# One quarter of the first modulation columns is moved between two products of the second weight pair

## The chip, the core and the metric

The kernel runs on one core of one Trainium2 chip. A core has a matrix engine (TensorE, PE in the profile; its weight loads are shown apart as PEld), a vector engine (VectorE, DVE), a scalar engine (ScalarE, ACT), a general engine (GpSimd, POOL) and a queue that issues transfers (SyncE, SP). Each engine works through its own instructions in order and waits for the others by semaphores. The metric is the device time of one execution in microseconds (us); less is better.

## The reference, cut to what matters

One decoder layer is computed for 512 prompt tokens and for 64 sample tokens (8 sequences of 8), all with 1024 features. Nine vectors c (one for the prompt, eight for the samples) give, through the matrix `w_ada`, nine chunks of 1024 modulation values; the first two chunks, `sh1` and `sc1`, are the shift and scale of the first feed-forward block.

```python
m = jax.nn.silu(c) @ w_ada + b_ada
sh1, sc1, g1, sh2, sc2, g2, sh3, sc3, g3 = jnp.split(m[:, None, :], N_MOD, axis=-1)
h = modulate(rms_norm(x, n1_g), sh1, sc1)          # n * (1 + scale) + shift
x = x + 0.5 * g1 * swiglu(h, w1_gate, w1_up, w1_down)
...                                                 # token mixing, then a second feed-forward block
```

`swiglu` is `(silu(h @ w_gate) * (h @ w_up)) @ w_down` with 2816 hidden columns, all in float32.

## The kernel before

**Layout.** Activations lie with features on the 128 partitions, in 8 chunks of 128 features, and with the 576 tokens as columns; the columns are cut into two halves of 288. Weights are taken 128 columns at a time, one block of `w_gate` and the same block of `w_up`; such a couple is a "pair". To keep float32 accuracy each operand is split into a high and a low part (ACT makes the high part, DVE the low part), and a product is three matmuls for each chunk: high by high, high by low, low by high. The function `prod` is one product over four chunks: 12 matmuls with 288 columns (profile line L651).

**Blocks.** The features are cut into an upper half (chunks 0 to 3) and a lower half (4 to 7), the tokens into two halves; this gives operand blocks such as N11 (upper features, first tokens, negated), N1 (a difference of the upper blocks), B21 and B22 (the lower features), and sums T2, N3, N4 for later pairs. Index j in a step's name is which two chunks: the steps ending in 0, 1 work on the upper half, the B21 and B22 steps ending in 2, 3 on the lower half. The steps ending in `h` plus a number write the high part on ACT (L564, L566), those in `l` the low part on DVE (L571, L575). The first two weight pairs, `pairs[0]` and `pairs[1]` of class `Plain`, use four steps of two products each:

- `h0a`: the pair's two weight blocks n11 (gate) and n21 (up) by N11, into two PSUM banks `A`;
- `snaps` (`sn0`, `sn1`): ACT copies both banks aside (L660);
- `h1a`: the same weights by N1, into two banks `D`;
- `h0b`: the blocks a12 and a22 by B21, added into `A`; `h1b`: the same by B22, added into `D`.

There are eight PSUM banks.

**The first modulation columns.** They come in four quarters, class `First`, each 256 columns of `sh1` and 256 of `sc1`. Quarter 3 serves the feature chunks 6 and 7. Each quarter has eight loads of 256 KB (L363) and four steps: `mm` is 16 matmuls on PE over the eight weight tiles (L307), `M` an ACT copy of the result from PSUM (L313), `tr` four transposes on PE (L319), and `m` three DVE instructions that finish the values (L324, L328, L387). With them the steps `b30` and `b31` (ACT, L540) and `s3` (DVE, L549) modulate the chunks 6 and 7, and only then can `N3c1` (DVE, L591), `B21h3` (ACT) and `B21l3` (DVE) make the last part of B21, and `B22h3` and `B22l3` that of B22. The weight tiles of quarter 3 lie in buffers that the operand blocks N3 (pool `xs1`, the tiles 0 to 3 of the quarter) and N4 (pool `xa`, the tiles 4 to 7) take over.

**The order.** The first stage is written out by hand in the string `BEGIN`: each word is a step. The function `run` calls the steps in this order and then adds a dependency between each instruction and the one before it on the same engine, for all engines but SP, so the order of the words is the order on PE, ACT, DVE and POOL. After `BEGIN` come the remaining pairs in a stream. Weight loads are issued by SP as buffers come free.

Of the kernel before, what the change touches and what calls it, by code (L numbers as in the profile page):

```python
# [44 lines left out]
xt0 xt1 xc0 xt2 xc1 xt3 xc2 xt4 xc3 s5 xt5 xc4 r5 r50 r51 r52 xt6 dg xc5 xt7 xc6 rw xS xc7  # L45
rr xr0 xr3 mm0 xr2 M0 tr0 xr1 mm1 m0 nh0 s0 M1 nl0 b00 tr1 b01 m1 wh0 tx0 b10 s1 b11 wl0
N11h0 N11h1 N11l0 N1h0 N11l1 mm2 tx1 N1l0 N1h1 h0a0 T2a1 M2 N1l1 nh1 T2a0 wh1 nl1 tr2 sn0
h1a0 m2 wl1 b20 b21 s2 B21h2 T2b0 B22h2 h0a1 B21l2 T2h0 N3c0 N4c0 N3h0 T2l0 N4h0 N3l0 mm3
B22l2 sn1 N4l0 M3 tr3 h1a1 m3 b30 s3 b31 B21h3 N3c1 p2ah B21l3 T2b1 h0b1 B22h3 p2al p2bh
T2h1 N3h1 N4c1 B22l3 N4h1 p2S h0b0 T2l1 p2U p2bl p2Sh N3l1 h1b0 p2V N4l1 p2Sl e0s0 e0s1 e0m0  # L50
e0m1 h1b1 e1a0 p2Uh e1t0 e1s0 p2Ul e1m0 Gh0 P1 e1a1 e1t1 e1s1 Gl0 P2 e1m1 P1s Gh1 Gl1 P5 P6
P5s P6s
# [32 lines left out]
def layer_kernel(ctx: ExitStack, tc: tile.TileContext, a):  # L85
# [24 lines left out]
    def nm(s):  # L110
        count[0] += 1
        return f"{s}_{count[0]}"
# [5 lines left out]
    def pool(stack, name, side="left"):  # L118
        return stack.enter_context(tc.tile_pool(name=nm(name), bufs=1, side=side, reuse_waits="tile"))
# [14 lines left out]
    def nine(home, shape, dt=F32R):  # L134
        return now[home].tile(shape, dt, tag="x", name=nm(home), bufs=4 if home == "xa" else 3)
# [9 lines left out]
    def bank():  # L145
        return pp.tile([P, 512], F32, tag="ps", name=nm("ps"), bufs=8)
# [85 lines left out]
    def tick(us):  # L232
        for s in list(side):
            s[1] -= us
            while s in side and s[1] <= 0:
                try:
                    s[1] += next(s[0])
                except StopIteration:
                    side.remove(s)
# [239 lines left out]
    def proj(w, X, h, kc=KC, c0=0, ks=None, ps=None):  # L479
        ps = bank() if ps is None else ps  # L480
        wh, wl = w
        for k in ks or range(kc):
            xh, xl = X[k]
            for z, (s, m) in enumerate(((wh, xh), (wh, xl), (wl, xh))):
                PE.matmul(  # L485
                    ps[:, :PW[h]], lhsT=s[:, k, c0:c0 + P], rhs=m[:, PART[h]],
                    start=k == 0 and z == 0, stop=k == kc - 1 and z == 2,
                )
        return ps
# [5 lines left out]
    def cost(kc):  # L495
        return kc * 3 * 0.1225
# [20 lines left out]
    def op(name):  # L517
        if name not in ops:
            t = nine("xs1" if name in ops["near"] else "xa", [P, 4, 2, H])
            ops[name] = t[:, :, 0], t[:, :, 1]  # L520
        return ops[name]
# [71 lines left out]
    def operand_steps(O):  # L593
        st = {}
        for j in range(2):
            for n in ("T2", "N3", "N4", "N1"):
                st[f"{n}h{j}"] = lambda n=n, j=j: O.hi(n, j)
                st[f"{n}l{j}"] = lambda n=n, j=j: O.lo(n, j)
            for n in ("B21", "B22"):
                st[f"{n}h{j + 2}"] = lambda n=n, j=j: O.hi(n, j)  # L600
                st[f"{n}l{j + 2}"] = lambda n=n, j=j: O.lo(n, j)
            st[f"N11h{j}"] = lambda j=j: O.hi("N11", j)
            st[f"N11l{j}"] = lambda j=j: O.lo("N11", j)
            st[f"tx{j}"] = lambda j=j: O.tx(j)
            for n in ("T2a", "T2b", "N3c", "N4c"):
                st[f"{n}{j}"] = lambda n=n, j=j: O.sums(n, j)
        for p in range(4):
            st[f"s{p}"] = lambda p=p: O.s(p)
        return st
# [14 lines left out]
    def pair_steps(p, greg):  # L624

        st = {}

        def G(i, f):
            if now.get("slf") is not greg:
                greg.close()  # L630
                now["sl"], now["slots"], now["slf"] = pool(greg, "slf", "right"), FSLOT, greg
            f(i)

        for i in range(2):
            for n, f in (("nh", "nh"), ("nl", "nl"), ("wh", "wh"), ("wl", "wl"), ("h0a", "h0a"), ("sn", "snaps"),
                         ("h1a", "h1a"), ("h0b", "h0b"), ("h1b", "h1b"), ("e0s", "e0s"), ("e0m", "e0m"),
                         ("e1a", "e1a"), ("e1s", "e1s"), ("e1t", "e1t"), ("e1m", "e1m")):
                st[f"{n}{i}"] = lambda i=i, f=f: getattr(p[i], f)()
            st[f"Gh{i}"] = lambda i=i: G(i, lambda i: p[i].finish_hi())
            st[f"Gl{i}"] = lambda i=i: G(i, lambda i: p[i].finish_lo())  # L640
        for n in ("p2ah", "p2al", "p2bh", "p2bl", "p2S", "p2Sh", "p2Sl", "p2U", "p2V", "p2Uh", "p2Ul"):
            st[n] = lambda n=n: getattr(p[2], n[2:])()
        for n, f in (("P1", "p1"), ("P2", "p2"), ("P5", "p5"), ("P6", "p6"), ("P1s", "p1s"), ("P5s", "p5s"), ("P6s", "p6s")):
            st[n] = lambda f=f: getattr(p[2], f)()
        return st

    def prod(ps, w, x, fresh):
        (wh, wl), (xh, xl) = w, x
        for j in range(4):
            for z, (s, m) in enumerate(((wh, xh), (wh, xl), (wl, xh))):  # L650
                PE.matmul(  # L651
                    ps[:, :H], lhsT=s[:, j * P:(j + 1) * P], rhs=m[:, j, :],
                    start=fresh and j == 0 and z == 0, stop=j == 3 and z == 2, skip_group_check=True,
                )
        tick(cost(4))
# [44 lines left out]
    class Plain(Weights):  # L700
# [21 lines left out]

        def h0a(self):
            self.A = [bank() for _ in range(2)]
            for ps, w in zip(self.A, ("n11", "n21")):
                prod(ps, self.w[w], op("N11"), True)

        def snaps(self):
            self.s = [snap(ps, half() if self.n and i else None) for i, ps in enumerate(self.A)]
# [294 lines left out]
    def cols(w, f):  # L1024
        return (w[0], f * P), (w[1], f * P)

    pairs = {0: Plain(cols(w1, 0), 0)}
# [14 lines left out]
    def turn_x(c):  # L1042
        psX[c] = bank()
        for n in range(4):
            PE.transpose(
                psX[c][:, n * P:(n + 1) * P], in_=xtok[n, c // 4][:, (c % 4) * P:(c % 4 + 1) * P], identity=ident
            )
        PE.transpose(
            psS[:, c * NS:(c + 1) * NS], in_=xtok[4, c // 4][:, (c % 4) * P:(c % 4 + 1) * P],
            identity=ident[0:NS, 0:NS],  # L1050
        )
# [37 lines left out]

    ops["near"] = ("B21", "B22", "N3")  # L1090
    steps = {**operand_steps(Late()), **pair_steps(pairs, greg)}
    for c in range(KC):
        steps[f"xt{c}"] = lambda c=c: turn_x(c)
        steps[f"xc{c}"] = lambda c=c: DVE.tensor_copy(out=xs[c][:, 0:NP], in_=psX[c])
# [733 lines left out]
    for pr in ([0], [1], [2], [3], [4], [5], [6, 7]):  # L1828
# [4 lines left out]
        for h in range(2):  # L1833
            for c in pr:
                ps = proj(W[c], OA, h)
# [44 lines left out]
    pairs = {0: Plain(cols(w2, 0), 0), 1: Plain(cols(w2, 1), 1), 2: Pair(cols(w2, 2))}  # L1880
    steps = {**operand_steps(O), **pair_steps(pairs, greg)}
# [173 lines left out]
```

## Time and profile before

| | |
|---|---|
| time, median of 3 runs | 1647.48 us (1645.12, 1647.48, 1648.8) |
| the profiled execution's own time | 1648.44 us |
| its span, first to last instruction | 1646.7 us |
| mean granted PE clock | 0.996 |
| PE busy | 1617.6 us, 98% of the span |
| PEld busy | 1554.9 us, 94% |
| DVE busy | 1152.2 us, 70% |
| ACT busy | 782.9 us, 48% |
| POOL busy | 293.0 us, 18% |

In a timeline a row is: start in us, length in us, engine, line, operation, output and inputs, shapes and count; in brackets at the end the engine's idle time ahead of the row and what is taken to have released it. Neighbouring instructions of one form are merged into one row, and since matmuls are pipelined the end of a merged row of PE can lie past the start of the next. The chain of waits is followed back from the last instruction to what released each step. A view by windows gives for each stretch of the span its length, the busy time of PE, PEld, DVE, ACT and POOL (number of instructions in brackets), the granted PE clock (1.00 is full), the busy share of the DMA engines and the GB/s that they moved. A named releaser is inferred from semaphore events; it can be a transfer that ended at the right moment while the true releaser was another.

### The profile page before, as it was taken

Reading aid. Unit: us, or ns where it says so; the run is one execution under the profiler, and the core shown is the slowest. Engines: PE = TensorE matmul, PEld = TensorE weight load, DVE = VectorE, ACT = ScalarE, POOL = GpSimd, SP = SyncE. Lnnn points to the kernel's source line nnn. Section 1 sums busy time; section 2 is a strip of 40 time slices with the busy share of each in tenths; the row PEclk is TensorE's granted clock in tenths of the full one; section 3 lists DMA queues with packets and bytes.
Section 4 is the critical chain, followed back from the end, with each engine's and each line's share of the span. In section 5 each row is a group of like instructions: output and inputs, shape, how many; then the busy total and the mean of one; then the engine's idle time right before and its main releaser. Section 6 shows DMA issues by size and latency. Waiting matters only on the chain.

```text
span 1646.7 us, 31365 instructions
## 1 busy us (share of the span) xinstructions
PE 1617.6 (98%) x12548; PEld 1554.9 (94%) x12548; DVE 1152.2 (70%) x1835; ACT 782.9 (48%) x1331; POOL 293.0 (18%) x372
## 2 busy tenths in 40 slices
PE   7999999999999999999999999999999999999997
PEld 4899999999999999999999999998999999999997
DVE  6867856676797877755688554676848868676773
ACT  5544524344664556554444453453236525343454
POOL 0000000000411101113346343454231000000002
PEclk9999999999999999999999999999999999999999
DMA  9453444332637676765457574799540333332331
GB/s 305 137 161 110 142 128 137 110 114 84 187 124 221 208 229 190 223 197 173 137 190 249 172 179 154 215 257 273 171 142 14 87 93 97 94 94 82 99 89 59
DMA packets 300212, 252.09 MB, mean 153 GB/s; under 512 B 13593, under 2 KB 260633, under 8 KB 300066
## 3 DMA queue, kind: packets, MB, share of 16 engines
q1 hardware_dynamic: 284594, 206.76, 41.5%
q0 software_dynamic: 13168, 40.97, 8.8%
q10 hardware_dynamic: 2304, 2.36, 0.4%
q8 instruction: 98, 1.61, 0.4%
q14 instruction: 48, 0.39, 0.1%
HBM read 207.01 MB, written 43.02 MB: 152 GB/s over the span
## 4 chain that ended last, share of the span: by engine, by line
PE 81%; DVE 8%; DMA 5%; ACT 3%; issue 2%; POOL 1%; SPq 0%; POOLq 0%; ACTq 0%; DVEq 0%
PE ps L651 36%; PE ps L485 29%; PE ps L1353 5%; PE ps L1583 3%; PE ps L307 2%; DVE whl L679 1%; DMA wraw<-in_w_down_dram 1%; ACT whl L669 1%; PE ps L1483 1%; DMA wraw<-in_w_a_dram 1%; DMA xa<-in_w_ada_dram 1%; PE ps L1445 1%; PE ps L1366 1%; PE ps L1489 1%; DVE xa L575 0%
## 5 line engine op out<-in xcount | busy, mean ns | idle before, releaser
L651 PE MATMUL ps<-xa,whl 128*128 128x288 f32 x3000 | 420.7, 295 | 3.5 <-DVE whl L679 1.6
L651 PEld LDWEIGHTS ps<-xa,whl 128*128 128x128 f32 x3000 | 401.7, 189 | 16.3 <-issue 3.4
L651 PE MATMUL ps<-xs,whl 128*128 128x288 f32 x2040 | 287.0, 294 | 1.3 <-ACT sn L660 1.3
L651 PEld LDWEIGHTS ps<-xs,whl 128*128 128x128 f32 x2040 | 272.0, 188 | 11.6 <-issue 5.0
L679 DVE TENSOR_TENSOR whl<-wraw,whl 128x1024 fp32r<-128x1024 f32 x192 | 234.4, 1222 | 55.5 <-ACT whl L669 46.9
L669 ACT CAST whl<-wraw 128x1024 fp32r<-128x1024 f32 x192 | 200.0, 1047 | 109.9 <-DVE wraw L793 67.9
L485 PEld LDWEIGHTS ps<-c,wd 128*128 128x128 f32 x1824 | 236.7, 188 | 3.5 <-issue 3.4
L485 PE MATMUL ps<-c,wd 128*128 128x320 f32 (+1 forms) x1824 | 239.8, 292 | 0.0
L485 PE MATMUL ps<-c,whl 128*128 128x256 f32 (+1 forms) x1368 | 186.9, 294 | 1.1 <-ACT c L195 0.7
L485 PEld LDWEIGHTS ps<-c,whl 128*128 128x128 f32 x1368 | 179.5, 188 | 3.3 <-ACT c L195 0.9
L472 POOL TENSOR_TENSOR x<-x,s 128x64 f32<-128x64 f32 x72 | 37.8, 526 | 793.8 <-DVE s L471 767.9
L466 DVE SCALAR_TENSOR_TENSOR x<-ps,gate,x 128x320 f32<-128x320 f32 (+1 forms) x128 | 61.0, 481 | 111.5 <-PE ps L485 111.2
L660 ACT COPY sn<-ps 128x288 f32<-128x288 f32 x195 | 76.9, 398 | 102.4 <-PE ps L651 102.1
L188 DVE TENSOR_TENSOR whl<-wraw,whl 128x1024 fp32r<-128x1024 f32 x56 | 76.4, 1365 | 65.5 <-ACT whl L187 64.8
L952 ACT CAST wd<-wraw 128x640 fp32r<-128x640 f32 (+2 forms) x58 | 45.4, 783 | 103.9 <-PE ps L485 97.4
L1353 PE MATMUL ps<-whl,xx 128*128 128x256 f32 x768 | 88.9, 276 | 0.0
L1353 PEld LDWEIGHTS ps<-whl,xx 128*128 128x128 f32 x768 | 88.0, 188 | 0.0
L651 PE MATMUL ps<-xs,whs 128*128 128x288 f32 x480 | 69.1, 292 | 0.0
L187 ACT CAST whl<-wraw 128x1024 fp32r<-128x1024 f32 x56 | 58.6, 1050 | 21.4 <-PE ps L485 13.4
L651 PEld LDWEIGHTS ps<-xs,whs 128*128 128x128 f32 x480 | 64.8, 188 | 0.0
L669 ACT CAST whs<-wraw 128x512 fp32r<-128x512 f32 x62 | 38.4, 620 | 54.5 <-PE ps L651 45.5
L957 DVE TENSOR_TENSOR wd<-wraw,wd 128x640 fp32r<-128x640 f32 (+2 forms) x58 | 53.4, 921 | 11.3 <-ACT wd L952 11.2
(285 smaller groups left out, 2215.9 us busy)
## 6 DMA issues: line engine op xcount, KB each, us to landing
ada<-in_w_ada_dram SPq DMA_DIRECT2D x56, 512.0 KB
wraw<-in_w_in_dram SPq DMA_DIRECT2D x96, 256.0 KB
wraw<-in_w_gate_dram SPq DMA_DIRECT2D x88, 256.0 KB
wraw<-in_w_up_dram SPq DMA_DIRECT2D x88, 256.0 KB
wraw<-in_w_in_dram SPq DMA_DIRECT2D x32, 512.0 KB
wraw<-in_w_down_dram SPq DMA_DIRECT2D x32, 384.0 KB
wraw<-in_w_down_dram SPq DMA_DIRECT2D x32, 320.0 KB
accd<-c POOLq DMA_DIRECT2D x32, 288.0 KB, 5.6
```

Of the source, the lines that this page charges most:

```text
L187: ACT.copy(out=hi, in_=raw)
L188: now["lo"] = (eng or DVE).tensor_tensor(out=lo, in0=raw, in1=hi.bitcast(F32), op=ALU.subtract)
L466: DVE.scalar_tensor_tensor(out=x[:, o:o + w], in0=ps[:, :w], scalar=g[:, c, 0:1], in1=x[:, o:o + w], op0=ALU.mult, op1=ALU.add)
L485: PE.matmul(ps[:, :PW[h]], lhsT=s[:, k, c0:c0 + P], rhs=m[:, PART[h]], start=k == 0 and z == 0, stop=k == kc - 1 and z == 2,)
L651: PE.matmul(ps[:, :H], lhsT=s[:, j * P:(j + 1) * P], rhs=m[:, j, :], start=fresh and j == 0 and z == 0, stop=j == 3 and z == 2, skip_group ...
L660: ACT.copy(out=t, in_=ps[:, :H])
L669: ACT.copy(out=hl[:, 0], in_=src)
L679: now["lo"] = DVE.tensor_tensor(out=hl[:, 1], in0=src, in1=hl[:, 0].bitcast(F32), op=ALU.subtract)
L952: ACT.copy(out=hl[:, 0], in_=self.raw[c])
L957: DVE.tensor_tensor(out=lo, in0=self.raw[c], in1=hi.bitcast(F32), op=ALU.subtract)
L1353: PE.matmul(ps[:, :DV], lhsT=s, rhs=m, start=i == 0, stop=i == 23)
L1583: PE.matmul(ps[:, :256], lhsT=s, rhs=m[:, kx % 4, :], start=kx == 0 and y == 0, stop=kx == KC - 1 and y == len(terms) - 1,)
```

## The change

The step `h0a1`, two products of `pairs[1]`, is split into `h0x1` (both banks are taken, the gate product) and `h0y1` (the up product). The words of quarter 3 are moved: `mm3` now stands ahead of `N3h0` and of `h0y1`, `M3` ahead of `h0y1`, `N4h0` and `sn1`. So on PE the order was gate product, up product, `mm3`, `tr3`, and is gate product, `mm3`, up product, `tr3`; on ACT it was `T2h0`, `N3h0`, `N4h0`, `sn1`, `M3`, and is `T2h0`, `N3h0`, `M3`, `N4h0`, `sn1`; on DVE it was `T2l0`, `N3l0`, `B22l2`, `N4l0`, `m3`, and is `T2l0`, `B22l2`, `N3l0`, `N4l0`, `m3`. From `tr3` on the words are as before.

```diff
-h1a0 m2 wl1 b20 b21 s2 B21h2 T2b0 B22h2 h0a1 B21l2 T2h0 N3c0 N4c0 N3h0 T2l0 N4h0 N3l0 mm3
-B22l2 sn1 N4l0 M3 tr3 h1a1 m3 b30 s3 b31 B21h3 N3c1 p2ah B21l3 T2b1 h0b1 B22h3 p2al p2bh
+h1a0 m2 wl1 b20 b21 s2 B21h2 T2b0 B22h2 h0x1 B21l2 T2h0 N3c0 N4c0 mm3 N3h0 T2l0 M3 h0y1 B22l2
+N4h0 N3l0 sn1 N4l0 tr3 h1a1 m3 b30 s3 b31 B21h3 N3c1 p2ah B21l3 T2b1 h0b1 B22h3 p2al p2bh
...
         def h0a(self):
             self.A = [bank() for _ in range(2)]
-            for ps, w in zip(self.A, ("n11", "n21")):
-                prod(ps, self.w[w], op("N11"), True)
+            for i in range(2):
+                self.h0(i)
+
+        def h0(self, i):
+            prod(self.A[i], self.w[("n11", "n21")[i]], op("N11"), True)
+
+        def h0x(self):
+            self.A = [bank() for _ in range(2)]
+            self.h0(0)
+
+        def h0y(self):
+            self.h0(1)
...
+    steps.pop("h0a1")
+    steps["h0x1"], steps["h0y1"] = pairs[1].h0x, pairs[1].h0y
```

## The prediction

> **What bounds the kernel now.** I read the totals first, then the chain of waits around the moved steps, then each engine's timeline there, and last the clock by windows. The page's head:
>
> ```profile
> span 1646.7 us, 31365 instructions
> PE 1617.6 (98%) x12548; PEld 1554.9 (94%) x12548; DVE 1152.2 (70%) x1835; ACT 782.9 (48%) x1331; POOL 293.0 (18%) x372
> ```
>
> PE is busy for all but 29.1 us of the span, so a microsecond taken from PE's idle time can reach the end. The profiled execution took 1648.44 us, 1.74 more than its span, and 0.96 more than the median of the runs. The chain from 45 us on:
>
> ```profile
> 42.34 5.60 DMA wraw<-in_w_gate_dram
> 47.94 0.65 ACT xa L566
> 48.59 0.30 ACT sn L660
> 48.89 0.30 ACT h L660
> 49.19 0.50 ACT ada L313
> 49.73 0.66 PE ps L319 x4
> 50.39 29.66 PE ps L651 x216
> ```
>
> Between 47.94 and 49.73 the chain leaves PE and runs through ACT (`N4h0`, `sn1`, `M3`); afterwards it is PE without a gap to 80 us. The first row I don't believe. PE's timeline and ACT's:
>
> ```profile
> 45.85 1.07 PE L307 MATMUL ps<-xs,cs 128*32 128x512 f32 x8
> 46.74 1.04 PE L307 MATMUL ps<-xa,cs 128*32 128x512 f32 x8
> 49.73 0.66 PE L319 MATMUL ps<-ident,ada 128*128 128x128 f32 x4 [1.96 <-ACT ada L313]
> 50.14 4.95 PE L651 MATMUL ps<-xa,whl 128*128 128x288 f32 x24
> 54.93 12.64 PE L651 MATMUL ps<-xs,whl 128*128 128x288 f32 x96
> 67.41 1.72 PE L651 MATMUL ps<-xa,whl 128*128 128x288 f32 x12
> ...
> 47.06 0.67 ACT L566 CAST xs<-hb 128x576 fp32r<-128x576 f32 x1 [2.99 <-DMA wraw<-in_w_gate_dram]
> 47.92 0.67 ACT L566 CAST xa<-hb 128x576 fp32r<-128x576 f32 x1 [0.19 <-DMA wraw<-in_w_gate_dram]
> 48.50 0.39 ACT L660 COPY sn<-ps 128x288 f32<-128x288 f32 x1
> 49.08 0.60 ACT L313 COPY ada<-ps 128x512 f32<-128x512 f32 x1
> 51.21 1.52 ACT L540 ACTIVATE hb<-hb,mT,a 128x512 f32<-128x512 f32 x2 [1.53 <-DVE a L387]
> ```
>
> ACT's 47.06 is `N3h0`, 47.92 `N4h0`. The page gives both waits to a transfer of gate weights, which neither step reads. But N3 takes over the buffer of quarter 3's weight tiles 0 to 3, N4 that of tiles 4 to 7, and `mm3` reads the first until 45.85 + 1.07 = 46.92 and the second until 46.74 + 1.04 = 47.78: each step starts 0.14 us after that. So the loop is: `mm3` holds up `N3h0` and `N4h0`; `M3`, fourth behind them, starts 1.30 us after `mm3`'s end; PE waits for `M3` with nothing else to do: **1.95 us idle**, 47.78 to 49.73.
>
> **A second loss follows it.** 96 matmuls take 67.41 - 54.93 = 12.48 us, 0.130 each; the 24 of `h1a1` take 54.93 - 50.14 = 4.79 instead of 3.12. The clock by windows, in PE busy and PEclk (the number ahead of the DMA share):
>
> ```profile
> 26.50:29.90 3.40, 1.98 (x14) 0.56 (x6) 3.11 (x10) 2.90 (x5) 0.00 (x0) 1.00 1.11 339
> 47.00:50.40 3.40, 1.45 (x14) 0.67 (x7) 2.09 (x3) 2.43 (x5) 0.00 (x0) 1.00 1.08 334
> 50.40:53.80 3.40, 3.40 (x16) 3.40 (x16) 2.30 (x7) 2.56 (x4) 0.00 (x0) 0.50 0.62 184
> 1286.00:1289.40 3.40, 1.61 (x10) 1.39 (x11) 3.40 (x5) 3.38 (x4) 0.00 (x0) 1.00 0.00 0
> 1289.40:1292.80 3.40, 3.40 (x16) 3.40 (x16) 3.33 (x5) 0.40 (x1) 0.00 (x0) 0.50 0.84 239
> ```
>
> From 50.4 to 53.8 the clock is granted at half: 4.79 - 3.12 = **1.67 us lost**. The same comes at 1289.4. Each time the 3.4 us just before held PE busy for under half (1.45 and 1.61); after 1.98 busy nothing came. I read the idle as its cause.
>
> **The change, part by part.** No instruction is added or removed: the same 24 matmuls, 16, and 4 transposes, in another order.
>
> *PE.* `h0x1` ends 12 x 0.130 = 1.56 before 45.85, at 44.29. `mm3` then takes its 1.93 (45.85 to 47.78) to 46.22, `h0y1` to 47.78. PE's work up to `tr3` is the same, so `tr3` can start at 47.78 if `M3` is ready. Passing from L651 to L307 and on costs no PE idle in the rows above; I take nothing for the two more changes of kind.
>
> *ACT.* `N3h0` starts when the first eight of `mm3` are done: 44.29 + 1.07 + 0.14 = 45.50, ending 46.17. `M3` starts 0.14 after `mm3`, 46.36, and ends 46.96: 0.82 ahead of the 47.78 at which PE asks for it. `h0y1`'s 1.56 us is the cover; without it `M3` would cost 0.74. `N4h0` runs behind `M3`, to about 47.6, `sn1`'s second copy starts after `h0y1`, 47.9, and ends at 48.3, ahead of `b30`, which moves from 51.21 to 49.3.
>
> *DVE.*
>
> ```profile
> 47.77 1.43 DVE L575 TENSOR_TENSOR xs<-hb,xs 128x576 fp32r<-128x576 f32 x2 [1.73 <-ACT xs L566]
> 49.11 0.75 DVE L575 TENSOR_TENSOR xa<-hb,xa 128x576 fp32r<-128x576 f32 x1
> 50.42 0.31 DVE L324 TENSOR_REDUCE m<-ps 128x36 f32<-128x144 f32 x1 [0.56 <-PE ps L319]
> 53.46 0.76 DVE L575 TENSOR_TENSOR xs<-hb,xs 128x576 fp32r<-128x576 f32 x1
> ```
>
> `N3l0`, `B22l2` and `N4l0` are the first three of these. `B22l2` goes ahead into the 1.73 us that DVE waits, `N4l0` follows `N4h0` at 47.6 and ends by 48.4; `m3` needs DVE at 47.78 + 0.69 (50.42 less 49.73) = 48.47. It fits. `tr3`, `m3`, `b30`, `b31` and `B21l3` all come **1.95 sooner**.
>
> *The weights.* `mm3` now asks for its last tile at 44.29 + 0.46 (its second set of weight loads starts 46.31 - 45.85 behind the first):
>
> ```profile
> 37.76 1.06 ACT L669 CAST whl<-wraw 128x1024 fp32r<-128x1024 f32 x1 [0.30 <-DMA wraw<-in_w_up_dram]
> 37.80:41.00 3.20, 3.20 (x27) 3.20 (x26) 1.95 (x5) 2.26 (x4) 0.00 (x0) 1.00 0.98 335
> 41.00:44.20 3.20, 3.20 (x27) 3.20 (x26) 3.06 (x6) 2.90 (x5) 0.00 (x0) 1.00 1.14 330
> 46.31 0.13 PEld L307 LDWEIGHTS ps<-xa,cs 128*32 128x32 f32 x4 [0.30 <-issue]
> ```
>
> The loads issued ahead of quarter 3's are in when `wh1` starts, 37.76. From there 335 and 330 GB/s over 3.2 us each move 2.13 MB by 44.20; quarter 3 is 8 x 262144 bytes = 2.10 MB. So its last tile is in at about 44.1 (an estimate, if loads land in the order of issue) and is wanted at 44.75: margin 0.6. The rows' other bound is 46.31, when the weights were used without a wait; then 1.56 of the gain would go. I take nothing, since the transfers' own rate is the nearer row. SP's next load (of a later strip, waiting for `tr3`) also moves up, with nothing that needs it soon.
>
> *What is late next.* With the clock full, PE reaches `h0b1` 3.62 sooner, but `B21l3` only 1.95. `B21l3` ended at 53.46 + 0.76 = 54.22, 4.49 after `tr3` began; now 52.27, and a semaphore step later 52.35. PE starts `h0b1` at 47.78 + 0.41 (50.14 less 49.73) + 3.12 = 51.31, and its eighth matmul, the first to read that low part, comes at 52.22: late by **0.1 to 0.15**. If the first matmul waits for the whole operand, it is 1.04. Which of the two, quarter 2's eight weight loads show (first and last of them):
>
> ```profile
> 29.40 0.14 PEld L307 LDWEIGHTS ps<-xs,cs 128*32 128x32 f32 x2 [0.39 <-DMA xs<-in_w_ada_dram]
> ...
> 34.81 0.14 PEld L307 LDWEIGHTS ps<-xs,cs 128*32 128x32 f32 x2 [0.64 <-DMA xs<-in_w_ada_dram]
> ```
>
> Four slices share a tile there, yet PE starts on each slice as it lands, 5.41 / 7 = 0.77 us apart. So I take 0.15. Further on there is room: `P1` (67.41) moves to about 63.9, and the bank that it needs is freed by `e0s0`, whose work also comes 1.95 sooner:
>
> ```profile
> 62.41 0.71 ACT L746 ACTIVATE g<-ps 128x288 f32<-128x288 f32 x2
> ```
>
> 62.41 + 0.71 - 1.95 = 61.2, 2.7 ahead.
>
> *Sum:* 1648.44 - 1.95 - 1.67 + 0.15 = **1644.97** for an execution like the profiled one, the later half-clock stretch still in it, and 1643.30 for one without that.
>
> [...]
>
> **Rivals.** *Only the idle goes* (0.20): the clock drop isn't this idle's, or is missing from most executions anyway. For it: the three times are 3.68 apart, about two such stretches, so they don't come up each time. Against: the windows above. Time 1647.48 - 1.95 = 1645.5. [...]
>
> *The next operand takes part back* (0.12): `h0b1` waits 1.04, not 0.15: 0.89 over the forecast below, 1645.3. For it: the 0.1 us that separate the two; against, the slice-wise waits.
>
> *Slower: the weights aren't there* (0.06). PE stops in `mm3` at 44.75 until the last tile lands, with `h0y1`, `tr3` and everything else behind it. Up to 0.6 us later than I place it nothing happens; past 44.75 + 1.95 = 46.70 the whole idle has only changed its place, and half clock follows it again. Landing at 47.2 would give 1648.0. Against: 46.31 above, and the transfers ahead are unchanged.
>
> *It doesn't do what it says* (0.05): ACT's order or a buffer's release still holds `M3` behind `N4h0` and `sn1`; 1647.5. Another 0.05 is for a larger gain, the later stretch at 1289.4 falling away through the shift: 1643 or less.
>
> **How the numbers follow.** The forecast holds 0.52. For its time I count a half-clock stretch as coming up in two of three executions: the kernel before is then 1648.44 - 2 x 1.67/3 = 1647.33, near its median of 1647.48. After: 1644.97 - 1.67/3 = **1644.4**, 3.1 us or 0.19% less, with an own range of 1643.3 to 1645.2. The range that leaves out 2 in 10 runs from 1642.7 (the larger gain) to 1646.9 (most of the margin in weights or clock lost). A measurement of this kernel tells about 0.2% (3.3 us) from no change, so faster means under 1644.2: 0.30 of the forecast's 0.52 (the later stretch comes up in no more than a third of the timed runs, or the runs before had more of them than I count), the larger gain's 0.05 and 0.08 of the two cases between (0.32), 0.43. Slower by over 0.2% takes a landing past 50 us or a cause that I don't see: 0.07. The rest, 0.50, is within.
>
> **What would show it.** Right: PE idle ahead of `tr3` (L319 near 47.8) under 0.2; `M3` starting about 46.4, ahead of `N4h0`; `N3h0` near 45.5; granted clock 1.00 from 48 to 54; `h0b1` near 51.3 with at most 0.2 of idle inside; P1 near 63.9. Wrong: a wait of L307 for its weights near 44.8; half clock in that stretch though the idle is gone; idle of 0.9 or more ahead of `h0b1`; or PE's gain at 64 us, 3.5, not found at the end of the span.

## The result, and the profile after

The changed kernel takes 1644.8 us in the median of 22 runs (1643.05 to 1648.7), the kernel before 1647.38 us in 22 runs beside it (1645.12 to 1650.46). The ratio is 0.9982, with an interval from 0.9976 to 0.9987: 0.18% faster, 2.6 us by the medians. The profiled execution of the changed kernel took 1643.43 us, with a span of 1641.6 us and a mean granted clock of 0.998. One later execution of the kernel before, at a mean granted clock of 0.657, took 2276.9 us and is left out of the comparisons.

The chain of waits of the changed kernel over the same stretch (start, length, what):

```profile
44.19 1.85 PE ps L307 x16
46.04 1.76 PE ps L651 x12
47.80 0.44 PE ps L319 x4
48.24 28.22 PE ps L651 x216
```

It no longer leaves PE: product, `mm3`, product, transposes, and then the 216 matmuls. Before, three ACT steps stood between `mm3` and the transposes. The timelines of PE and ACT of the changed kernel:

```profile
44.12 1.06 PE L307 MATMUL ps<-xs,cs 128*32 128x512 f32 x8
45.00 1.04 PE L307 MATMUL ps<-xa,cs 128*32 128x512 f32 x8
45.97 1.83 PE L651 MATMUL ps<-xa,whl 128*128 128x288 f32 x12
47.64 0.60 PE L319 MATMUL ps<-ident,ada 128*128 128x128 f32 x4
48.00 3.37 PE L651 MATMUL ps<-xa,whl 128*128 128x288 f32 x24
51.21 4.97 PE L651 MATMUL ps<-xs,whl 128*128 128x288 f32 x36
...
63.82 1.72 PE L651 MATMUL ps<-xa,whl 128*128 128x288 f32 x12
...
45.33 0.67 ACT L566 CAST xs<-hb 128x576 fp32r<-128x576 f32 x1 [1.38 <-PE ps L307]
46.19 0.59 ACT L313 COPY ada<-ps 128x512 f32<-128x512 f32 x1 [0.19 <-PE ps L307]
46.67 0.67 ACT L566 CAST xa<-hb 128x576 fp32r<-128x576 f32 x1
```

The transposes begin at 47.64 without idle, 2.09 us sooner than before's 49.73. `N3h0` now starts at 45.33, and the page itself names PE's L307, `mm3`, as its releaser, no longer a transfer. `N4h0` comes at 46.67, behind `M3`. `h1a1` takes 51.21 - 48.00 = 3.21 us where it took 4.79. By windows (PEclk ahead of the DMA share), the changed kernel:

```profile
44.66:48.08 3.42, 3.42 (x33) 2.28 (x26) 3.30 (x5) 2.37 (x5) 0.00 (x0) 1.00 1.19 297
48.08:51.49 3.41, 3.41 (x29) 3.41 (x28) 2.19 (x8) 2.56 (x5) 0.00 (x0) 1.00 1.07 371
```

PE is busy throughout, and the clock is full. At `P1` the changed kernel is 67.41 - 63.82 = 3.59 us ahead. The spans differ by 5.1: most of the other 1.5 us comes at the second half-clock stretch, which the profiled execution before had at 1289.4 and this one has not. Its window there (busy PE is the first number behind the comma):

```profile
1280.29:1283.70 3.41, 2.03 (x16) 1.80 (x15) 3.32 (x7) 2.54 (x5) 0.00 (x0) 1.00 0.01 2
```

The change doesn't touch that place, so this part isn't counted as its gain; the next section tells what decides.

### The profile page after: what moved, and what is told of

It reads as the page before. It is cut to its first block, busy times and chain, and to the rows that moved or that the text cites. A ratio compares the mean times of both kernels' runs of the same rounds, so it can differ in the third digit from the quotient of the medians.

```text
span 1641.6 us, 31367 instructions
## 1 busy us (share of the span) xinstructions
PE 1613.3 (98%) x12548; PEld 1551.7 (95%) x12548; DVE 1152.0 (70%) x1835; ACT 782.6 (48%) x1331; POOL 292.9 (18%) x372
## 4 chain that ended last, share of the span: by engine, by line
PE 81%; DVE 8%; DMA 4%; ACT 3%; issue 2%; POOL 1%; SPq 0%; POOLq 0%; DVEq 0%; ACTq 0%
PE ps L651 36%; PE ps L485 30%; PE ps L1365 5%; PE ps L1595 3%; PE ps L307 2%; DVE whl L679 1%; DMA wraw<-in_w_down_dram 1%; ACT whl L669 1%; PE ps L1495 1%; PE ps L1457 1%; DMA xa<-in_w_ada_dram 1%; PE ps L1378 1%; PE ps L1501 1%; DMA ada<-in_w_ada_dram 0%; DVE xa L575 0%
```

## The experiments

My theory: the gain is PE's 1.95 us of idle and, in some executions, a half-clock stretch that this idle brings on. The rivals: the idle alone; or the place of `M3` on ACT, or of `mm3` on PE, by itself.

**The copy put back, `mm3` left.** In the changed kernel:

```diff
-mm3 N3h0 T2l0 M3 h0y1 B22l2 N4h0 N3l0 sn1 N4l0 tr3
+mm3 N3h0 T2l0 h0y1 B22l2 N4h0 N3l0 sn1 N4l0 M3 tr3
```

> The changed kernel with M3 put back behind N4h0 and sn1 on ACT; mm3 stays between the two products. sn1's second copy waits for the up product's end (47.7), M3 then runs 48.13 to 48.73 and tr3 starts at 48.8 in place of 47.64. Theory (the copy must lie under the up product): 1.0 to 1.1 us of PE idle and a time 1.05 us over the changed kernel, about 1645.8; half clock seldom, as the idle is short. Rival (mm3's place alone brings the gain, since it frees N3's and N4's buffers): as the changed kernel, 1644.8.

The second half of `mm3` in this kernel, `N4h0` behind it, PE's row for the transposes, then its row at 751 us:

```profile
45.84 1.04 PE L307 MATMUL ps<-xa,cs 128*32 128x512 f32 x8
47.02 0.67 ACT L566 CAST xa<-hb 128x576 fp32r<-128x576 f32 x1 [0.19 <-PE ps L307]
49.62 0.66 PE L319 MATMUL ps<-ident,ada 128*128 128x128 f32 x4 [0.98 <-ACT ada L313]
...
751.40 1.16 PE L1395 MATMUL ps<-c,c 128*128 128x128 f32 x8 [2.02 <-POOL c L1343]
```

The idle is 0.98 us, near the 1.0 to 1.1 expected, and the clock stays full. The median fell short: 1647.39 us in 11 runs, beside 1647.90 for the kernel before in 33 (ratio 0.9994, 0.9985 to 1.0003), some 0.5 under before where 1.6 was expected. The interval reaches from 2.5 under to 0.5 over, so the miss isn't resolved. This kernel's profile shows a wait that can hide part of the gain: at 751 us, where the retention begins, PE waits 2.02 us for POOL where the kernel before waits 1.20 and the changed one 1.16. All instructions from `tr3` on stand in the same order in these kernels. That the copy has to lie under the up product is shown by PE's idle, which comes back with `mm3` still in its new place; the time is in keeping but doesn't show it by itself.

**Only the copy moved.** In the kernel before:

```diff
-N3c0 N4c0 N3h0 T2l0 N4h0 N3l0 mm3 B22l2 sn1 N4l0 M3 tr3
+N3c0 N4c0 mm3 M3 N3h0 T2l0 N4h0 N3l0 B22l2 sn1 N4l0 tr3
```

> The kernel before with PE's order kept (both products, then mm3) and only M3 put ahead of N3h0, N4h0 and sn1 on ACT. tr3 then starts at 48.6, 1.15 us sooner, with 0.8 us of idle left; but N3h0 and N4h0 run behind M3, N4l0 ends at 51.2, m3 comes 0.75 us later than before, and h0b1's eighth matmul waits about 2 us for B21l3, until 55. Theory (the buffers that mm3 holds set N3 and N4, and m3 stands behind them on DVE, so the copy alone wins nothing): 1647.1 to 1648.2, no gain over before. Rival (the copy's place on ACT is what counts): 1.15 us and the half-clock share sooner, about 1645.4.

PE's timeline of this kernel:

```profile
48.51 0.66 PE L319 MATMUL ps<-ident,ada 128*128 128x128 f32 x4 [0.78 <-ACT ada L313]
48.92 1.82 PE L651 MATMUL ps<-xa,whl 128*128 128x288 f32 x12
51.43 1.85 PE L651 MATMUL ps<-xa,whl 128*128 128x288 f32 x12 [0.69 <-DVE m L324]
53.12 1.42 PE L651 MATMUL ps<-xs,whl 128*128 128x288 f32 x7
54.93 1.32 PE L651 MATMUL ps<-xs,whl 128*128 128x288 f32 x8 [0.39 <-DVE xs L575]
```

The transposes come 1.2 us sooner, and all of it and more is given back: 0.69 us in the middle of `h1a1`, and about 0.9 ahead of the eighth matmul of `h0b1` (54.93, where seven matmuls of 0.130 from 53.12 would have ended at 54.03). The median is 1648.45 us, before 1647.90 (1.0003, 0.9994 to 1.0012). So the copy's place on ACT is worth nothing without `mm3`'s: N3 and N4 stay behind `mm3`, and `m3` behind `N4l0` on DVE. The 0.69 us I had not foreseen: the second product of `h1a1` takes the bank that `tr3` wrote, and `m3`'s first instruction (L324) must have read it (the page names L324 as the releaser; that it is this bank is inferred).

**`mm3` ahead of both products.** It shows when the weights land:

```diff
-B22h2 h0x1 B21l2 T2h0 N3c0 N4c0 mm3 N3h0 T2l0 M3 h0y1 B22l2
+B22h2 mm3 h0a1 B21l2 T2h0 N3c0 N4c0 N3h0 T2l0 M3 B22l2
```

> mm3 put ahead of both products of the second pair (h0a1 whole again behind it), M3 ahead of N4h0 and sn1: PE asks for quarter 3's weights at 42.6, before they are in, so the profile shows when the last tile lands. Theory (last tile in at about 44.1): PE's second set of L307 weight loads waits until 44.1, some 0.6 to 1.0 us of idle; tr3 near 48.3; a time 0.6 to 0.9 us over the changed kernel. Rival (weights later than placed, the margin in the changed kernel nearly nothing): landing at 44.6 or later and 1.2 us or more over it; rival (weights long in): no wait, as the changed kernel.

The weight loads and the matmuls of L307 in this kernel:

```profile
42.82 0.12 PEld L307 LDWEIGHTS ps<-xa,cs 128*32 128x32 f32 x3 [0.30 <-issue]
43.25 0.28 PEld L307 LDWEIGHTS ps<-xa,cs 128*32 128x32 f32 x5 [0.30 <-issue]
...
42.36 1.07 PE L307 MATMUL ps<-xs,cs 128*32 128x512 f32 x8
43.25 1.19 PE L307 MATMUL ps<-xa,cs 128*32 128x512 f32 x8
```

Only one of the second set's loads is held back, by 0.14 us, and the second eight matmuls take 1.19 us in place of 1.04: the last tile is in only just too late for them, at some 43.4. My 44.1 was 0.7 too late, and the changed kernel, which asks at 44.6, has over a microsecond of margin in this execution. The time is 1644.86 us beside 1644.60 of the changed kernel (11 runs each): the order of `mm3` and the first product can't be told apart. What counts is a product behind `mm3` and ahead of `tr3`. This profile has one half-clock stretch that the profiles before and after haven't, at 28.8, behind an idle of 1.99 us in the stage ahead.

**The idle filled.** In the kernel before, 14 matmuls between `mm3` and `tr3`:

```diff
+p2 = bank()
+for i in range(14):
+    PE.matmul(p2[:, :H], lhsT=pairs[1].w["n11"][0][:, 0:P], rhs=op("N11")[0][:, 0, :],
+              start=i == 0, stop=i == 13, skip_group_check=True)
...                                   # then tr3's four transposes into p2
```

> The kernel before with 14 extra matmuls of 288 columns on PE between mm3 and tr3 (1.82 us, into the bank that the transposes then overwrite), so that PE isn't idle there and nothing is moved. Theory (half clock comes from the idle): PE still reaches tr3 at 49.73, the clock stays at 1.00 from 50.4 to 53.8, and the time falls by 1.67 us in the executions that had the stretch, 0.8 to 1.1 us in the median: about 1646.4 beside 1647.4. Rival (the idle's 1.95 us are all there is): no change, 1647.4.

> The kernel before with 14 extra matmuls ahead of tr3, a second time, for more runs. Theory (the half-clock stretch follows PE's idle): mean time 0.8 to 1.1 us under before and the mean clock 0.0005 to 0.0007 over it. Rival (the clock drop has nothing to do with this idle, or costs nothing on average): before's mean time, within 0.4.

PE's rows in the first of the two, and its rows at 752 and 753 us in the first and in the second:

```profile
47.98 2.11 PE L1115 MATMUL ps<-xa,whl 128*128 128x288 f32 x14
50.02 0.65 PE L1121 MATMUL ps<-ident,ada 128*128 128x128 f32 x4
50.42 3.38 PE L651 MATMUL ps<-xa,whl 128*128 128x288 f32 x24
...
751.78 1.16 PE L1397 MATMUL ps<-c,c 128*128 128x128 f32 x8 [2.51 <-POOL c L1345]
```

```profile
753.33 1.16 PE L1397 MATMUL ps<-c,c 128*128 128x128 f32 x8 [2.45 <-POOL c L1345]
```

The gap is filled, `tr3` comes 3.9 us after `mm3` began, as before, and `h1a1` runs at full clock in both. But the time didn't follow: 1647.54 us beside 1647.90 (0.9998, 0.9989 to 1.0007), and the second time 1649.53 beside 1647.60 (1.0011, 1.0002 to 1.002), slower, which neither the theory nor its rival allowed for. The first interval still holds the 0.8 to 1.1 us of the theory as well as no change. In both profiles the wait for POOL is 1.3 us longer than before's 1.20; in the second a half-clock stretch follows it, at 754.6, and PE idles 1.13 us at 389, which the first doesn't. So this experiment doesn't show in the time what the half clock costs.

What sets that wait can be read one step further back. POOL's instruction stands behind a chain of DVE and POOL instructions, and the first of these, by the page, waits for a load. Its row before, and in the first filled kernel:

```profile
744.04 0.75 DVE L1327 TENSOR_TENSOR c<-c,rope 64x576 f32<-64x576 f32 x1 [5.04 <-DMA rope<-in_rope_dram]
743.19 0.75 DVE L1341 TENSOR_TENSOR c<-c,rope 64x576 f32<-64x576 f32 x1 [6.38 <-DMA rope<-in_rope_dram]
```

PE resumes 8.59 us after this row in both (752.63 and 751.78), and 8.6 us after it in all eleven profiles of kernels without made idles. From the issue of the `rope` load, which it reads, to this row it takes 6.1 to 6.2 us in seven of the eleven, 6.6 in one of the kernel before, 7.0 with the copy put back and 7.4 to 7.5 in the two of the filled kernel, and PE's wait is longer by as much. So the chain isn't slower; it starts later, with the loads. Why they come later is open, and one program differs from itself in this.

**The clock counted over many executions.** The kernel before and the changed one, unchanged, once more:

> The kernel before, unchanged, to see its clock in many executions. Theory (part of the gain is a half-clock stretch that follows the 1.95 us of PE idle in some executions): over the runs the mean granted clock is lower than after's (0.998 in 10 of 22 runs, 0.997 in 11, 0.996 in one), about one step of 0.001 in about half of them, since 3.4 us at half clock are 0.001 of the span; the gain of 2.6 to 2.7 us is then 1.95 + 0.5 x 1.67 - 0.13. Rival (idle alone, the rest is noise): the same clocks as after's.

> The changed kernel again, beside the kernel before on the same chip, for the clock of both. Theory (idle and half clock): 2.6 to 2.8 us faster than before; its mean granted clock over the runs is higher than before's by 0.0005 to 0.0010, half to all of one 3.4 us stretch. Rival (idle alone): 1.8 us faster and the same mean clock.

The changed kernel again: 1644.60 us beside 1647.60 (0.9983, 0.9974 to 0.9992), mean clock 0.9975 beside 0.9968. The kernel before against itself: 1647.54 and 1647.90 us, with mean clocks of 0.9971 and 0.9964. One program differs from itself by 0.36 us and 0.0007, the latter as much as the two kernels do from each other in their run, so the mean clock decides nothing. Two single profiles of the kernel before were plainer:

> The kernel before, unchanged, for one more profile of the stretch behind the 1.95 us of idle. Theory: half clock from about 50.4 in about half of the profiles; where it is missing, h1a1's 24 matmuls take 3.1 to 3.2 us in place of 4.79.

> As b1_look, one more profile of the kernel before: half clock behind the idle in about half of them.

PE's rows in the first of them:

```profile
45.26 1.06 PE L307 MATMUL ps<-xs,cs 128*32 128x512 f32 x8
...
49.14 0.66 PE L319 MATMUL ps<-ident,ada 128*128 128x128 f32 x4 [1.96 <-ACT ada L313]
49.55 3.37 PE L651 MATMUL ps<-xa,whl 128*128 128x288 f32 x24
52.77 12.78 PE L651 MATMUL ps<-xs,whl 128*128 128x288 f32 x96
65.39 1.72 PE L651 MATMUL ps<-xa,whl 128*128 128x288 f32 x12
```

In both the idle of 1.96 us is there, and no half clock follows; `h1a1` takes 52.77 - 49.55 = 3.22 and 53.81 - 50.60 = 3.21 us. So it came in one of three profiles.

**Many idles in one execution.** They show what decides. The changed kernel, with this ahead of each later `p5`, and the products held in their written order:

```diff
+m1 = PE.matmul(ps[:, :H], lhsT=x[:, 0:P], rhs=x, start=True, stop=True, skip_group_check=True)
+for i in range(k):                    # k = 5; in the second kernel 2 and 9 in turn
+    ACT.copy(out=t, in_=ps[:, :H])
+m2 = PE.transpose(ps[:, 0:P], in_=t[:, 0:P], identity=ident)
```

> The changed kernel with PE made idle on purpose in each later pair of both feed-forward blocks and of the mixing projections, ahead of the pair's p5: one extra matmul, five ACT copies of 288 columns that follow it, and a transpose that waits for them, all other products kept in their written order; nothing else is changed and nothing left out. About 55 idles of near 2 us in one execution. Theory (an idle of the size that the change removes is followed by half clock for 3.4 us in some of the cases, by where it falls): a third to two thirds of them are. [...] Rival (always): all.

> The same with two and nine copies in turn, idles of near 1 us and near 3.2 us. Theory: of the short ones under one in ten is followed by half clock, of the long ones nine in ten or more. Rival (a busy share under half in the 3.4 us before is not what decides): short and long alike.

The idles came out longer than planned, most of them 2.6 to 3.6 us with five copies. 42 of the 57 made idles were followed by half clock, more than the two thirds expected of idles near 2 us. In the second kernel it was 3 of the 27 made idles up to 2.3 us, where under one in ten was expected, and all 26 over 4 us. So half clock doesn't always follow. Of all idles over 0.4 us in the two profiles (after 60 us), this many are followed by half clock: under 1.5 us, 0 of 25; 1.5 to 2.3 us, 3 of 17; 2.3 to 3.0 us, 9 of 22; 3.0 to 3.7 us, 29 of 38; longer, 39 of 39. Length alone doesn't decide: two idles of the first kernel, both 3.59 us, in windows of 3.41 us counted on from the first half-clock stretch:

```profile
178.89:182.30 3.41, 1.68 (x13) 1.45 (x12) 2.35 (x4) 2.83 (x5) 0.00 (x0) 1.00 0.52 154
182.30:185.71 3.41, 1.54 (x12) 1.55 (x13) 3.31 (x6) 1.68 (x5) 0.00 (x0) 1.00 0.00 0
185.71:189.12 3.41, 3.41 (x27) 3.29 (x26) 0.57 (x2) 1.75 (x3) 0.00 (x0) 1.00 0.02 5
...
213.02:216.43 3.41, 0.69 (x5) 0.69 (x6) 3.23 (x5) 2.54 (x7) 0.00 (x0) 1.00 0.17 49
216.43:219.84 3.41, 3.41 (x17) 3.41 (x16) 1.34 (x2) 0.40 (x1) 0.00 (x0) 0.50 0.00 0
```

The first idle is split by a window's edge; PE is busy 1.68 and 1.54 us in the two windows, and the clock stays full. The second lies almost in one window, 0.69 busy, and the next window is at half. All the half-clock stretches of each of these two profiles begin on one grid of 3.413 us and, but for the last behind the matmuls' end, last one to three of its windows. Of the 1006 windows that the clock's record of these two profiles has at full (it begins at 22 to 23 us, and the window ahead of the last stretch isn't counted), 80 were followed by half clock, with PE busy 0.00 to 0.47 of the window, and 926 were not, with 0.44 or more. The kernel before fits, in windows set by its own stretch, and so does the second of its two single profiles:

```profile
46.98:50.39 3.41, 1.46 (x14) 0.66 (x7) 2.09 (x3) 2.43 (x5) 0.00 (x0) 1.00 1.08 333
50.39:53.80 3.41, 3.41 (x16) 3.41 (x16) 2.30 (x7) 2.56 (x4) 0.00 (x0) 0.50 0.63 184
```

```profile
46.05:49.46 3.41, 2.18 (x19) 0.51 (x17) 1.74 (x3) 1.76 (x4) 0.00 (x0) 1.00 1.19 312
49.46:52.87 3.41, 2.69 (x21) 2.69 (x22) 2.12 (x7) 1.88 (x4) 0.00 (x0) 1.00 0.71 220
```

In the first the whole idle lies in one window, 1.46 / 3.41 = 0.43 busy. In the other an edge splits the idle into windows of 0.64 and 0.79, and nothing follows. The later place fits too. Two idles, of 1.38 and 0.83 us, stand there alike in ten of the profiles; the window with most of them was busy 0.35 to 0.51 in the six that have the later stretch and 0.59 or 0.60 in the four that haven't, the changed kernel's first profile (2.03 / 3.41) among these.

**The other place filled.** The changed kernel with 10 matmuls ahead of the product that waits near 1282 us:

```diff
 self.D = bank()
+x = op("N11")[0][:, 0, :]
+for i in range(10):
+    PE.matmul(self.D[:, :H], lhsT=x[:, 0:P], rhs=x, start=i == 0, stop=i == 9, skip_group_check=True)
```

> The changed kernel with 10 extra matmuls of 288 columns on PE in the second feed-forward block, right ahead of the product that waits 1.38 us for its weights at 1282 us (1.3 us of them, into the bank that the product then overwrites). Theory (the other half-clock stretch, which the kernel before showed at 1289.4, follows that idle in about half of the executions): mean time 0.4 to 0.9 us under the changed kernel, mean clock 0.0003 to 0.0005 over its. Rival (idle there has nothing to do with the clock): as the changed kernel or up to 0.1 us slower.

Its PE rows there:

```profile
1282.33 1.35 PE L848 MATMUL ps<-xs 128*128 128x288 f32 x9
1283.74 0.80 PE L651 MATMUL ps<-xa,whl 128*128 128x288 f32 x4
1285.38 2.89 PE L651 MATMUL ps<-xa,whl 128*128 128x288 f32 x20 [0.83 <-DVE whl L679]
```

The 1.38 us of idle are gone, only 0.83 are left, and the clock stays full. The median is 1644.29 us beside 1644.60 of the changed kernel, 0.3 less where 0.4 to 0.9 were expected; against the kernel before the ratio is 0.9982 (0.9973 to 0.9991). The runs lie closer together, 1643.54 to 1644.86 where the changed kernel's eleven lie from 1643.15 to 1646.79. A gain over the changed kernel isn't resolved. The mean clock is 0.9980 beside 0.9975, as expected, but one program differs from itself by more; the smaller spread fits a stretch that came in some runs and now doesn't.

## Why the prediction was right, point by point

**The forecast**, 1644.4 us, is 0.4 under the measured 1644.8, and the gain was put at 3.1 us where the medians give 2.6. Its own terms, 1.95 - 0.15 + 2/3 x 1.67, give 2.9. The mechanism held; that the time came so near is in part luck, since the half clock's share rests on a frequency taken from one profile and the spread of three times.

**The loop.** That N3h0 and N4h0 waited for `mm3`'s buffers, not for a transfer, was right: moved, `N3h0` starts 0.15 us after `mm3`'s first half, and the page now names PE; `N4h0`, which the change puts behind `M3`, starts 0.14 us after the second half where the copy is put back (47.02, and 45.84 + 1.04 = 46.88). `mm3`, `M3`, `N3h0`, `tr3` and `h0b1` were placed at 44.29, 46.36, 45.50, 47.78 and 51.31; they came at 44.12, 46.19, 45.33, 47.64 and 51.21, all 0.1 to 0.2 sooner, as PE's whole first stage was in that execution.

**The idle, 1.95 us.** Right; with the copy put back, 0.98 of it return, as worked out.

**The next operand, 0.15 us.** Right in size: `h0b1` to `P1` takes 63.82 - 51.21 = 12.61 us, 0.13 over the 12.48 of 96 matmuls. PE waited by slices (with only the copy moved, 0.39 us ahead of the eighth matmul), so the rival with 1.04 us fell. But the kernel before pays this too when its clock stays full, 65.39 - 52.77 = 12.62 us; only its half clock hid it.

**The weights.** No wait, as taken, though the margin was over a microsecond and not 0.6. The rival that ended on the slower side had nothing behind it.

**The half clock, 1.67 us.** The mechanism was right, the idle brings it on; how often was not, and the size was a little too large. From `mm3`'s start to `P1` the kernel before takes 67.41 - 45.85 = 21.56 us with the stretch and 65.39 - 45.26 = 20.13 without: 1.43 us, since `h1a1` takes 3.21 and not 3.12 at full clock and the next operand is then late as well. I counted it in two of three executions; three profiles gave one. In the two profiles with made idles half clock came, from full clock, behind windows busy for 0.47 at most, and always behind those under 0.44. With 0.45 taken between them, at least 1.88 us of idle have to lie in one window; an idle of 1.96 us that may begin anywhere in a window does so in (3.41 - 1.96 + 2 x 0.08) / 3.41 = 0.47 of the cases (an estimate from these two profiles). The mean gain is then 1.95 + 0.47 x 1.43 = 2.6, again an estimate. It meets the difference of the medians, but the times don't prove it: their interval is 2.1 to 4.0 us, idle alone would give 1.95, and the experiment that filled the idle showed no gain. That the half clock follows the idle is shown by the windows; how much of the median it makes is not. I also read "under half busy" off windows that I had laid by the stretch itself; laid without it, such a window needn't have the effect: in the second single profile of the kernel before, PE is busy for 1.44 us from 47.0 to 50.4, an edge at 49.46 cuts the idle, and the clock stays full.

**Faster, same, slower.** The measured 0.18% lies within the 0.2% to which I gave 0.50.

## What to carry to other kernels

When one engine idles for a small copy, look for independent work of that engine that can stand between the work copied and the work that needs the copy; here one of two products was enough, and the split cost no idle of PE. Move the producer as well as the copy: the copy alone went nowhere (1648.45 us beside 1647.90), as the steps that waited for the producer's buffers were pushed behind it. Ask whose buffer a waiting step takes over before believing a named transfer, and count what an idle of TensorE costs in clock as a chance, not as certain: here half clock followed the 1.96 us in one of three profiles.

## What the runs showed of the hardware

A window's busy share told half clock more sharply than I had expected, though not quite sharply. In the two kernels with made idles the half-clock edges of a profile lie on one grid of 3.413 us (to 0.004 us); at full clock, windows with PE busy for up to 0.47 were followed by half, windows with 0.44 or more by full. From half clock the shares were others: of these profiles' 120 windows at half, the 40 that were followed by half again had PE busy 0.79 or less, the 80 that were followed by full clock 0.80 or more. These shares are PE's modelled busy time. In the other profiles a window of 0.51 (`mm3` ahead of both products, at 1281.5) was followed by half clock, and windows of 0.45, 0.48 and 0.51 were not (the second single profile of the kernel before at 25.6, the first filled kernel at 747.6, the second at 27.5). So between 0.44 and 0.51 this share doesn't tell.

An idle of 1.96 us sufficed in the profile before, and so did 12 of the 39 idles of 1.5 to 3.0 us in the two kernels with made idles.

Second, PE's wait for POOL at 750 us was 1.13 to 1.27 us in seven profiles, 1.64 in one of the kernel before, and 2.0 to 2.5 in three others that issue the same instructions there. It moved single profiles by up to half of the change's gain, and it goes back to the `rope` load, whose reader on DVE starts 6.1 to 7.5 us after the load's issue; POOL's name hides that.
